# The first adaLN modulation of a hybrid trunk, summed on TensorE with the weights as the stationary operand

## The chip, the cores and the metric

The kernel runs on one core of one Trainium2 chip. The metric is the device time of one execution in microseconds, as the median of several runs. The kernel before took 2763.83 us (three runs, 2754.28 to 2770.14).

## The reference, cut to what matters

Two layers run over 256 context tokens and 512 latent tokens of width 1024. Ahead of each layer a conditioning vector, one for the latent tokens and one for the context tokens, is turned into shifts, scales and gates by one large matrix:

```python
s_lat = jax.nn.silu(c)
s_ctx = jax.nn.silu(c_ctx)
for l in range(DEPTH):
    m_lat = jnp.split((s_lat @ w_mod[l] + b_mod[l])[:, None, :], 6, axis=-1)
    m_ctx = jnp.split((s_ctx @ w_mod[l] + b_mod[l])[None, None, :], 6, axis=-1)
    h_lat = _modulate(x_lat, m_lat[0], m_lat[1])     # x * (1 + scale) + shift
    h_ctx = _modulate(x_ctx, m_ctx[0], m_ctx[1])
    ...                                              # input projection, four mixers, merge, LayerNorm, MLP
```

`w_mod[l]` is 1024 x 6144 in fp32, so this is a product of two vectors with a 25 MB matrix. Of all twelve blocks of 512 columns, layer 0 needs four (shift and scale) before its first useful product can start; the other eight, and those of layer 1, are wanted later.

## The kernel before, in words

Features lie on the 128 partitions, tokens along the free dimension. The program is written with an automatic planner: it orders each engine's instructions by priority (mostly program order), by its own idea of when operands are ready, and by free buffers; on the chip every engine and the DMA-issuing queue of SyncE (SP) then work strictly in that order. One pool tag has a fixed number of buffers, and an instruction that needs one waits until an earlier tile of the tag is released.

The vectors are made in `modulation` (L429): `ccs` holds SiLU(c) as eight columns of 128 features, two vectors side by side. One block of 512 modulation columns is summed over four quarters of 256 rows each; a quarter is 128 partitions x 2 x 512 numbers, one load. `todo` (L438) is the list of (layer, block, quarter).

Two ways of summing a block stand in the program:

- on TensorE (`first_mod`, L471 on): the load goes to tile `modw` (tag `k4`, six buffers, which the later RWKV tiles `kpad`, `ktmp`, `kr` share). The two vectors are the stationary operand (128 x 2) and the weights stream past, 512 columns at a time (L486). The sum is two rows of 512; ScalarE copies them from PSUM to `modrow` (L489), and four products with a 2 x 2 identity turn them onto the partitions (L492, tile `pq`);
- on VectorE (`mod_unit`, L447): the load goes to tile `wraw` (three buffers, shared with all weight loads of the input projection), VectorE multiplies and adds over 512 columns four times a quarter into `modacc` (L458, L460), and 16 products with a column of ones sum over the partitions (L467).

`first_mod` takes the first 16 quarters of `todo` in two parts of two blocks. In part 0 five quarters go to TensorE and three to VectorE (`fm0=5`), in part 1 six and two (`fm1=6`); a block that is split between the engines gets two additions (`add_mod`, L495). After each part `first_h` (L584) loads four input tiles `xt` (L593), scales and shifts them on VectorE (L595) and splits them into `hhi` and `hlo` (L302, L303). The first product of the input projection, r0, needs all eight; its weights are loaded after part 0 (L521). `add_mod` of part 1 is thus the last thing ahead of the second half of r0, and everything later follows from there. Later blocks of the modulation go through `mod_unit` one by one, between other work (`mod_thread`, `more_mod`).

All fp32 products of this stage (not the fp32r ones on `hhi`, `hlo`) appear in the trace as two records each. PSUM tag `fp` has two buffers.

Of the kernel before, what the change touches and what calls it, by code (L numbers as in the profile page):

```python
# [137 lines left out]
def _layout(inp):  # L138
    g = {k: np.asarray(v) for k, v in inp.items()}
    a = {}  # L140
    tok = np.concatenate([g["ctx"][0], g["x"][0]], 0)
    a["xT"] = tok.T.reshape(8, 128, T).transpose(1, 0, 2)
    i2 = np.zeros((128, 1, 2), np.float32)
    i2[0:2, 0] = np.eye(2, dtype=np.float32)
    a["cc"] = np.concatenate([np.stack([g["c"][0], g["c_ctx"]], 1).reshape(8, 128, 2).transpose(1, 0, 2), i2], 1)
    a["wmod"] = g["w_mod"].reshape(DEPTH, 4, 2, 128, 12, 512).transpose(0, 4, 1, 3, 2, 5)
    cols = _inproj_columns()
    win = np.zeros((DEPTH, NIP, 128, 8, 128), np.float32)
# [42 lines left out]
    o = SMC["w2a2"][0]  # L191
# [3 lines left out]
    o = SMC["g2"][0]  # L195
# [25 lines left out]
    i = np.arange(128)  # L221
# [14 lines left out]

PARM = (
         dict(rw0=0.3, rw1=0.1, lru=1.7, mla0=2, mla1=0.7, mlp=0.462, ml0=0.66, ml1=0.785, ga=4, sp=3, g3=10,
              g1=0.462, mod=6.6, left=219, left0=136, hr=0, hm=0, hf=0, hw=50, fm0=5, fm1=6, cs=1, dl=1, nr=1, lns=2,
              hl0=0, hl1=0, hl2=0, hres=0, hx=0, pw1=146, pw2=2, mpos=0, mstart=0),  # L240
         dict(rw0=0.099, rw1=0.3, lru=2.8, mla0=1.96, mla1=1.705, mlp=2.38, ml0=2.785, ml1=2.36, ga=2, sp=1.18,
              g3=10, g1=0.809, mod=16.8, left=146, left0=0, hr=0, hm=0, hf=0, hw=50, fm0=5, fm1=6, cs=0, dl=1, nr=0,
              lns=2, hl0=0, hl1=0, hl2=0, hres=0, hx=0, pw1=0, pw2=0, mpos=3, mstart=60),
)

# [1 line left out]
class Trunk:  # L247
# [180 lines left out]

    def modulation(self):  # L429
        nc = self.nc  # L430
        cc = self.cp.tile([128, 9, 2], F32, name="ccs")
        nc.sync.dma_start(cc, self.ins["cc"])
        ccs = cc[:, 0:8, :]
# [6 lines left out]
        self.id2 = cc[0:2, 8, :]  # L440

    def more_mod(self, n):

        for _ in range(min(n, len(self.todo))):
            self.mod_unit(*self.todo.pop(0), 0, 3)

    def mod_unit(self, l, blk, q, first, last):  # L447
# [3 lines left out]
        if q == first:  # L451
            self.acc = [self.cp.tile([128, 512], F32, tag=f"modacc{v}", name="modacc") for v in range(2)]
        for j in range(2):
            w = raw[:, 512 * j:512 * j + 512]
            for v, acc in enumerate(self.acc):
                c = self.ccs[:, 2 * q + j, v:v + 1]
                if q == first and j == 0:
# [3 lines left out]
        if q == last:  # L461
# [7 lines left out]
            self.add_mod(l, blk, pq, first > 0)  # L469

    def first_mod(self, quarters):  # L471

        nc = self.nc
        units, self.todo = self.todo[:8], self.todo[8:]
        first = quarters - 4
        ps = [self.fp("pmod") for _ in range(1 + (first > 0))]
        for q in range(4):
            for i, (l, blk, _) in enumerate((units[q], units[4 + q])):
                end = (3, first - 1)[i]
                if q > end:  # L480
                    self.mod_unit(l, blk, q, first, 3)
                    continue
                raw = self.k4("modw", (128, 2, 512))
                nc.sync.dma_start(raw, self.ins["wmod"][l, blk, q])
                for j in range(2):
                    self.mm(ps[i][0:2, :], lhsT=self.ccs[:, 2 * q + j, :], rhs=raw[:, j], start=(q + j == 0), stop=(q == end and j == 1))  # L486
                if q == end:
                    row = self.k4("modrow")[0:2, 0:512]
                    nc.scalar.activation(row, ps[i][0:2, :], AF.Copy)  # L489
                    pq = self.fp("pq")  # L490
                    for c in range(4):
                        self.mm(pq[:, 2 * c:2 * c + 2], lhsT=row[:, 128 * c:128 * c + 128], rhs=self.id2, start=True, stop=True)  # L492
                    self.add_mod(l, blk, pq, False)

    def add_mod(self, l, blk, pq, more):  # L495
        o = VEC["b_mod"][0] + 4 * blk
        m = self.mods[l][:, 4 * blk:4 * blk + 4, :]
        self.nc.vector.tensor_tensor(m, pq[:, 0:8].rearrange("p (c v) -> p c v", v=2),
                                     m if more else self.vecs[l][:, o:o + 4].unsqueeze(2).to_broadcast([128, 4, 2]), op=ALU.add)


    def layer(self, l):
        nc, tc = self.nc, self.tc
        self.l = l
        full = self.full = l < DEPTH - 1
        self.parm = PARM[0 if self.full else 1]
        with ExitStack() as ctx:
            self.phase(ctx, False)
            self.vec = self.vecs[l]
            self.mod = self.mods[l]  # L510
            if l == 0:
                nc.sync.dma_start(self.vecs[0], self.ins["vec"][0])
                for part in range(2):
                    self.first_mod(self.parm[f'fm{part}'])
                    self.first_h(part)
                    if part == 1 - self.parm['cs']:
                        nc.sync.dma_start(self.cst, self.ins["cst"])
                        for j in range(1, self.depth):
                            nc.sync.dma_start(self.vecs[j], self.ins["vec"][j])
                    if part == 0:  # L520
                        self.ahead = {IP[i]: self.load_w(self.ins["win"][0, IP[i]]) for i in ("r0",)}  # L521
            self.derived()
            self.mixers()
# [1245 lines left out]
```

## Time and profile before

| | |
|---|---|
| median of three runs | 2763.83 us |
| lowest, highest | 2754.28, 2770.14 us |
| the profiled execution | 2754.58 us, of it the profile's span 2752.8 us |
| TensorE busy | 2591.9 us (94%) |
| VectorE, ScalarE, GpSimd busy | 1538.8, 1030.2, 445.6 us |
| HBM read, written | 261.21 MB, 34.52 MB |

Read it in this way: TensorE is busy for 94% of the span, so a change pays in general only if TensorE gets its next useful product sooner. The profile's slices are 68.8 us wide, and the whole stage that the change touches lies inside the first one, so the page's strips can't resolve it; it has to be read in windows of a few microseconds and in the time-ordered list of instructions.

### The profile page before, as it was taken

To read this page: it belongs to the slowest core of one execution; us is meant where nothing else is said; L and a number is where in the kernel's file an instruction comes from. 1 tells how busy PE (TensorE), PEld (TensorE's weight loads), DVE (VectorE), ACT (ScalarE), POOL (GpSimd) and SP (SyncE) were. 2 spreads that over 40 slices of the span, in tenths; PEclk is the share of its full clock that TensorE was granted. 3 is DMA by queue.
4 is the path that set the end of the run, shared out by engine and by line. 5 is a ranking of instruction groups with operands and counts; after the bars stand their busy time and mean duration, and the time that the engine had idled before them with its cause. 6 is when DMAs were issued, how large, how long until landed. Compare 5 with 4: busy or idle time off the path is not lost. (4 is left out here: it accounts for less than half of the span.)

```text
span 2752.8 us, 53610 instructions
## 1 busy us (share of the span) xinstructions
PE 2591.9 (94%) x22980; PEld 2116.0 (77%) x22980; DVE 1538.8 (56%) x2627; ACT 1030.2 (37%) x1642; POOL 445.6 (16%) x420
## 2 busy tenths in 40 slices
PE   7999999999989999999999989889999989999997
PEld 4777776778878878888888767666777867888887
DVE  6885776643353378555552575564665346833336
ACT  3653334343222244121212466543433333623334
POOL 0111112110132131020102200121201014211111
PEclk9999999999999999999999999999998989999999
DMA  7451331132362323434332242211212455333333
GB/s 261 155 188 51 98 96 46 37 93 86 96 232 74 122 86 121 126 120 124 122 123 73 85 144 100 74 52 55 71 53 78 128 170 200 112 106 93 99 93 107
DMA packets 117294, 299.30 MB, mean 109 GB/s; under 512 B 11024, under 2 KB 38032, under 8 KB 117056
## 3 DMA queue, kind: packets, MB, share of 16 engines
q1 hardware_dynamic: 117056, 295.87, 33.7%
q8 instruction: 180, 2.95, 0.4%
q14 instruction: 58, 0.48, 0.1%
HBM read 261.21 MB, written 34.52 MB: 107 GB/s over the span
## 5 line engine op out<-in xcount | busy, mean ns | idle before, releaser
L302 ACT ACTIVATE whi<-wraw 128x1024 fp32r<-128x1024 f32 x295 | 312.2, 1058 | 954.7 <-PE m L389 758.0
L389 PE MATMUL m<-hhi,whi 128*128 128x256 f32 (+1 forms) x2000 | 600.4, 361 | 14.0 <-ACT hhi L917 3.4
L389 PE MATMUL m<-hlo,whi 128*128 128x256 f32 (+1 forms) x2000 | 591.6, 357 | 3.6 <-DVE hlo L918 2.9
L389 PE MATMUL m<-hhi,wlo 128*128 128x256 f32 (+1 forms) x2000 | 588.3, 355 | 1.4 <-issue 1.0
L303 DVE TENSOR_TENSOR wlo<-wraw,whi 128x1024 fp32r<-128x1024 f32 x291 | 364.0, 1252 | 371.0 <-ACT whi L302 359.9
L389 PEld LDWEIGHTS m<-hhi,whi 128*128 128x128 f32 x2000 | 379.2, 191 | 77.0 <-issue 8.5
L389 PEld LDWEIGHTS m<-hlo,whi 128*128 128x128 f32 x2000 | 381.2, 191 | 59.6 <-DVE hlo L918 6.2
L389 PEld LDWEIGHTS m<-hhi,wlo 128*128 128x128 f32 x2000 | 380.3, 191 | 55.5 <-issue 3.4
L460 DVE SCALAR_TENSOR_TENSOR modacc<-wraw,ccs,modacc 128x512 f32<-128x512 f32 x296 | 222.5, 800 | 34.1 <-DMA wraw<-wmod 33.8
L815 POOL TENSOR_TENSOR rl<-rl 128x512 f32<-128x512 f32 (+2 forms) x73 | 116.3, 1593 | 706.9 <-ACT rl L814 655.6
L389 PE MATMUL m<-fhi,whi 128*128 128x256 f32 (+1 forms) x608 | 176.2, 341 | 1.2 <-ACT fhi L302 1.2
L389 PE MATMUL m<-flo,whi 128*128 128x256 f32 (+1 forms) x608 | 175.6, 340 | 0.2 <-DVE flo L303 0.2
L389 PE MATMUL m<-fhi,wlo 128*128 128x256 f32 (+1 forms) x608 | 174.8, 339 | 0.0
L791 DVE SCALAR_TENSOR_TENSOR x<-m,dvec,x 128x512 f32<-128x512 f32 (+1 forms) x92 | 53.8, 606 | 130.7 <-PE m L389 130.7
L389 PEld LDWEIGHTS m<-flo,whi 128*128 128x128 f32 x608 | 114.3, 188 | 14.5 <-DVE flo L303 0.6
L389 PEld LDWEIGHTS m<-fhi,whi 128*128 128x128 f32 x608 | 114.0, 188 | 14.7 <-ACT fhi L302 1.4
L389 PEld LDWEIGHTS m<-fhi,wlo 128*128 128x128 f32 x608 | 114.2, 188 | 13.9
L716 POOL TENSOR_TENSOR gth<-gth 128x768 f32<-128x768 f32 (+1 forms) x48 | 86.7, 1827 | 228.1 <-DVE gth L712 158.4
L389 PE MATMUL m<-osp,whi 128*128 128x512 f32 (+1 forms) x384 | 102.4, 374 | 17.3 <-ACT osp L302 10.1
L303 DVE TENSOR_TENSOR flo<-rl,fhi 128x512 fp32r<-128x512 f32 (+2 forms) x73 | 54.4, 745 | 84.7 <-ACT fhi L302 84.5
L389 PEld LDWEIGHTS m<-osp,whi 128*128 128x128 f32 x384 | 68.8, 195 | 36.0 <-ACT osp L302 12.1
L302 ACT ACTIVATE fhi<-rl 128x512 fp32r<-128x512 f32 (+2 forms) x73 | 49.1, 673 | 111.7 <-POOL rl L815 111.6
(425 smaller groups left out, 4355.8 us busy)
## 6 DMA issues: line engine op xcount, KB each, us to landing
wraw<-wf SPq DMA_DIRECT2D x145, 512.0 KB, 3.5
wraw<-win SPq DMA_DIRECT2D x106, 512.0 KB, 3.7
wraw<-wmod SPq DMA_DIRECT2D x85, 512.0 KB, 3.6
wraw<-wout SPq DMA_DIRECT2D x28, 512.0 KB, 3.8
kwin<-rkv SPq DMA_DIRECT2D x20, 512.0 KB, 5.3
gd<-gth SPq DMA_DIRECT2D x22, 384.0 KB, 3.4
gth<-gd SPq DMA_DIRECT2D x22, 384.0 KB, 5.3
wraw<-wbr SPq DMA_DIRECT2D x16, 512.0 KB, 4.5
```

The lines of the kernel that those rows point to most:

```text
L302: self.nc.scalar.activation(hi, src, AF.Copy)
L303: (self.nc.gpsimd if pool else self.nc.vector).tensor_tensor(lo, src, hi.bitcast(F32), op=ALU.subtract)
L389: self.nc.tensor.matmul(out, lhsT=lhsT, rhs=rhs, start=start, stop=stop)
L460: nc.vector.scalar_tensor_tensor(acc, w, c, acc, op0=ALU.mult, op1=ALU.add)
L716: nc.gpsimd.tensor_tensor(self.z[dt][:, q0:T], self.z[dt][:, q0:T], th[:, q0:T], op=ALU.add)
L791: nc.vector.scalar_tensor_tensor(x[et][:, a:b], ps[:, a + off:b + off], gm[:, et, j:j + 1], x[et][:, a:b], op0=ALU.mult, op1=ALU.add)
L815: nc.gpsimd.tensor_tensor(rl[:, a:b], rl[:, a:b], rl[:, a:b], op=ALU.mult)
```

## The change

All 16 quarters of the first modulation go to TensorE. The weights become the stationary operand, 64 columns at a time, and the two vectors (128 x 2) stream past: per quarter 2 x 4 x 2 = 16 products of 128 x 64 with 128 x 2, which add up in PSUM directly with the features on the partitions. The copy of the rows, the turning products, the 2 x 2 identity in the input `cc`, the share of VectorE (`first`, `last`, `fm0`, `fm1`) and the second addition go. Later blocks still go through `mod_unit`, unchanged.

```diff
-    a["cc"] = np.concatenate([np.stack([g["c"][0], g["c_ctx"]], 1).reshape(8, 128, 2).transpose(1, 0, 2), i2], 1)
+    a["cc"] = np.stack([g["c"][0], g["c_ctx"]], 1).reshape(8, 128, 2).transpose(1, 0, 2)
...
-    def first_mod(self, quarters):
+    def first_mod(self):
         nc = self.nc
         units, self.todo = self.todo[:8], self.todo[8:]
-        first = quarters - 4
-        ps = [self.fp("pmod") for _ in range(1 + (first > 0))]
+        ps = [self.fp("pmod") for _ in range(2)]
         for q in range(4):
-            for i, (l, blk, _) in enumerate((units[q], units[4 + q])):
-                end = (3, first - 1)[i]
-                if q > end:
-                    self.mod_unit(l, blk, q, first, 3)
-                    continue
+            for i in range(2):
+                l, blk, _ = units[4 * i + q]
                 raw = self.k4("modw", (128, 2, 512))
                 nc.sync.dma_start(raw, self.ins["wmod"][l, blk, q])
                 for j in range(2):
-                    self.mm(ps[i][0:2, :], lhsT=self.ccs[:, 2 * q + j, :], rhs=raw[:, j], start=(q + j == 0), stop=(q == end and j == 1))
-                if q == end:
-                    row = self.k4("modrow")[0:2, 0:512]
-                    nc.scalar.activation(row, ps[i][0:2, :], AF.Copy)
-                    pq = self.fp("pq")
                     for c in range(4):
-                        self.mm(pq[:, 2 * c:2 * c + 2], lhsT=row[:, 128 * c:128 * c + 128], rhs=self.id2, start=True, stop=True)
-                    self.add_mod(l, blk, pq, False)
+                        for e in range(2):
+                            o = 128 * c + 64 * e
+                            self.mm(ps[i][64 * e:64 * e + 64, 2 * c:2 * c + 2], lhsT=raw[:, j, o:o + 64], rhs=self.ccs[:, 2 * q + j, :],
+                                    start=(q + j + c == 0), stop=(q == 3 and j == 1 and c == 3))
+                if q == 3:
+                    self.add_mod(l, blk, ps[i])
...
-                    self.first_mod(self.parm[f'fm{part}'])
+                    self.first_mod()
```

## Rows read from the trace of the kernel before

**Rows 1.** The page, its first part: busy time of the engines over the span.

```profile
PE 2591.9 (94%) x22980; PEld 2116.0 (77%) x22980; DVE 1538.8 (56%) x2627; ACT 1030.2 (37%) x1642; POOL 445.6 (16%) x420
```

**Rows 2.** Long windows: stretch and its length, then busy us (and count) of PE, PEld, DVE, ACT, POOL, then PEclk, DMA share, GB/s.

```profile
0.00:48.65 48.65, 34.87 (x164) 13.52 (x164) 26.66 (x90) 13.74 (x20) 0.78 (x15) 0.92 0.83 318
48.65:54.00 5.35, 4.92 (x14) 3.93 (x15) 5.35 (x10) 3.30 (x4) 0.00 (x0) 0.50 0.00 0
...
60.00:80.00 20.00, 19.66 (x130) 15.96 (x129) 19.33 (x30) 9.67 (x12) 1.55 (x4) 1.00 0.58 188
```

**Rows 3.** Windows of 2 us in the first 50 us, columns as in group 2.

```profile
2.00:4.00 2.00, 0.00 (x0) 0.00 (x0) 0.00 (x0) 0.23 (x2) 0.00 (x0) 1.00 0.63 135
4.00:6.00 2.00, 0.17 (x1) 0.12 (x2) 1.15 (x13) 0.97 (x2) 0.00 (x0) 1.00 1.02 397
...
22.00:24.00 2.00, 0.11 (x4) 0.02 (x2) 1.84 (x10) 0.51 (x1) 0.00 (x0) 0.83 1.03 412
...
26.00:28.00 2.00, 2.00 (x3) 0.25 (x2) 2.00 (x3) 0.01 (x1) 0.00 (x0) 0.50 1.03 410
...
38.00:40.00 2.00, 2.00 (x13) 1.57 (x11) 1.72 (x3) 0.00 (x0) 0.00 (x0) 1.00 0.75 302
...
46.00:48.00 2.00, 0.40 (x14) 0.31 (x12) 1.52 (x6) 0.24 (x1) 0.00 (x0) 0.80 0.00 0
```

**Rows 4.** Timeline, first 50 us: start us, us, engine, line, operation, count, idle before and releaser.

```profile
5.83 5.48 PE L389 MATMUL pmod<-modw,ccs 128*2 128x512 f32 x8 [5.83 <-DMA modw<-wmod]
...
14.04 5.31 PE L389 MATMUL pmod<-modw,ccs 128*2 128x512 f32 x12 [1.00 <-DMA modw<-wmod]
...
21.01 1.10 PE L389 MATMUL pq<-one,modacc 128*64 128x1 f32 x32
...
25.84 9.15 PE L389 MATMUL pmod<-modw,ccs 128*2 128x512 f32 x16
...
36.98 2.74 DVE L460 SCALAR_TENSOR_TENSOR modacc<-wraw,ccs,modacc 128x512 f32<-128x512 f32 x4
...
40.05 3.59 PE L389 MATMUL pmod<-modw,ccs 128*2 128x512 f32 x8
...
43.68 0.59 ACT L489 ACTIVATE modrow<-pmod 2x512 f32<-2x512 f32 x1 [8.06 <-DMA lruw<-lruw]
...
44.32 1.05 PE L389 MATMUL pq<-ccs,modrow 2*128 2x2 f32 x8
...
45.30 1.10 PE L389 MATMUL pq<-one,modacc 128*64 128x1 f32 x32
...
46.45 0.17 DVE L498 TENSOR_TENSOR mod<-pq,mod 128x8 f32<-128x8 f32 x1 [0.87 <-PE pq L389]
...
48.65 1.01 PE L389 MATMUL m<-hhi,whi 128*128 128x256 f32 x2 [2.25 <-ACT hhi L302]
```

**Rows 5.** Timeline of the SP queue: start of issue, time in issue, line, tile, count.

```profile
22.20 7.58 SPq L484 DMA_DIRECT2D modw<-wmod  x2
...
33.21 2.64 SPq L450 DMA_DIRECT2D wraw<-wmod  x2
...
40.13 0.42 SPq L954 DMA_DIRECT2D lruw<-lruw  x1
55.88 0.33 SPq L450 DMA_DIRECT2D wraw<-wmod  x1
```

**Rows 6.** Loads of the first 70 us: line, size of one, median time to landing.

```profile
modw<-wmod SPq DMA_DIRECT2D x11, 512.0 KB, 11.1
...
xt<-xT SPq DMA_DIRECT2D x8, 384.0 KB, 8.0
...
cst<-cst SPq DMA_DIRECT2D x1, 865.0 KB
```

**Rows 7.** PE by shape at 2106 us, and the window with its granted clock, columns as in group 2.

```profile
L389 PE MATMUL kpx<-kS,kKR 64*64 64x64 f32 x16 | 1.1, 318 | 0.0
...
2106.00:2108.00 2.00, 2.00 (x26) 1.82 (x26) 0.74 (x3) 0.54 (x2) 0.00 (x0) 0.50 0.00 0
```

More of the change, by code (lines that the diff above doesn't have):

```diff
@@ L142, in _layout @@
     a["xT"] = tok.T.reshape(8, 128, T).transpose(1, 0, 2)
-    i2 = np.zeros((128, 1, 2), np.float32)
-    i2[0:2, 0] = np.eye(2, dtype=np.float32)
-    a["cc"] = np.concatenate([np.stack([g["c"][0], g["c_ctx"]], 1).reshape(8, 128, 2).transpose(1, 0, 2), i2], 1)
+    a["cc"] = np.stack([g["c"][0], g["c_ctx"]], 1).reshape(8, 128, 2).transpose(1, 0, 2)
     a["wmod"] = g["w_mod"].reshape(DEPTH, 4, 2, 128, 12, 512).transpose(0, 4, 1, 3, 2, 5)
@@ L238 @@
          dict(rw0=0.3, rw1=0.1, lru=1.7, mla0=2, mla1=0.7, mlp=0.462, ml0=0.66, ml1=0.785, ga=4, sp=3, g3=10,
-              g1=0.462, mod=6.6, left=219, left0=136, hr=0, hm=0, hf=0, hw=50, fm0=5, fm1=6, cs=1, dl=1, nr=1, lns=2,
+              g1=0.462, mod=6.6, left=219, left0=136, hr=0, hm=0, hf=0, hw=50, cs=1, dl=1, nr=1, lns=2,
               hl0=0, hl1=0, hl2=0, hres=0, hx=0, pw1=146, pw2=2, mpos=0, mstart=0),
          dict(rw0=0.099, rw1=0.3, lru=2.8, mla0=1.96, mla1=1.705, mlp=2.38, ml0=2.785, ml1=2.36, ga=2, sp=1.18,
-              g3=10, g1=0.809, mod=16.8, left=146, left0=0, hr=0, hm=0, hf=0, hw=50, fm0=5, fm1=6, cs=0, dl=1, nr=0,
+              g3=10, g1=0.809, mod=16.8, left=146, left0=0, hr=0, hm=0, hf=0, hw=50, cs=0, dl=1, nr=0,
               lns=2, hl0=0, hl1=0, hl2=0, hres=0, hx=0, pw1=0, pw2=0, mpos=3, mstart=60),
@@ L430, in modulation @@
         nc = self.nc
-        cc = self.cp.tile([128, 9, 2], F32, name="ccs")
-        nc.sync.dma_start(cc, self.ins["cc"])
-        ccs = cc[:, 0:8, :]
+        ccs = self.cp.tile([128, 8, 2], F32, name="ccs")
+        nc.sync.dma_start(ccs, self.ins["cc"])
         th = self.cp.tile([128, 8, 2], F32, name="ccth")
@@ L439, in modulation, with mod_unit @@
         self.ccs = ccs
-        self.id2 = cc[0:2, 8, :]
     def more_mod(self, n):
         for _ in range(min(n, len(self.todo))):
-            self.mod_unit(*self.todo.pop(0), 0, 3)
-    def mod_unit(self, l, blk, q, first, last):
+            self.mod_unit(*self.todo.pop(0))
+    def mod_unit(self, l, blk, q):
         nc = self.nc
@@ L450, in mod_unit @@
         nc.sync.dma_start(raw, self.ins["wmod"][l, blk, q])
-        if q == first:
+        if q == 0:
             self.acc = [self.cp.tile([128, 512], F32, tag=f"modacc{v}", name="modacc") for v in range(2)]
@@ L456, in mod_unit @@
                 c = self.ccs[:, 2 * q + j, v:v + 1]
-                if q == first and j == 0:
+                if q + j == 0:
                     nc.vector.tensor_scalar(acc, w, c, 0.0, op0=ALU.mult, op1=ALU.add)
@@ L460, in mod_unit @@
                     nc.vector.scalar_tensor_tensor(acc, w, c, acc, op0=ALU.mult, op1=ALU.add)
-        if q == last:
+        if q == 3:
             pq = self.fp("pq")
@@ L468, in mod_unit @@
                                 lhsT=acc[:, 128 * c + 64 * e:128 * c + 64 * e + 64], rhs=self.one, start=True, stop=True)
-            self.add_mod(l, blk, pq, first > 0)
-    def first_mod(self, quarters):
+            self.add_mod(l, blk, pq)
+    def first_mod(self):
         nc = self.nc
         units, self.todo = self.todo[:8], self.todo[8:]
-        first = quarters - 4
-        ps = [self.fp("pmod") for _ in range(1 + (first > 0))]
+        ps = [self.fp("pmod") for _ in range(2)]
         for q in range(4):
-            for i, (l, blk, _) in enumerate((units[q], units[4 + q])):
-                end = (3, first - 1)[i]
-                if q > end:
-                    self.mod_unit(l, blk, q, first, 3)
-                    continue
+            for i in range(2):
+                l, blk, _ = units[4 * i + q]
                 raw = self.k4("modw", (128, 2, 512))
@@ L485, in first_mod, with add_mod @@
                 for j in range(2):
-                    self.mm(ps[i][0:2, :], lhsT=self.ccs[:, 2 * q + j, :], rhs=raw[:, j], start=(q + j == 0), stop=(q == end and j == 1))
-                if q == end:
-                    row = self.k4("modrow")[0:2, 0:512]
-                    nc.scalar.activation(row, ps[i][0:2, :], AF.Copy)
-                    pq = self.fp("pq")
-                    for c in range(4):
-                        self.mm(pq[:, 2 * c:2 * c + 2], lhsT=row[:, 128 * c:128 * c + 128], rhs=self.id2, start=True, stop=True)
-                    self.add_mod(l, blk, pq, False)
-    def add_mod(self, l, blk, pq, more):
+                    for c in range(4):
+                        for e in range(2):
+                            o = 128 * c + 64 * e
+                            self.mm(ps[i][64 * e:64 * e + 64, 2 * c:2 * c + 2], lhsT=raw[:, j, o:o + 64], rhs=self.ccs[:, 2 * q + j, :],
+                                    start=(q + j + c == 0), stop=(q == 3 and j == 1 and c == 3))
+                if q == 3:
+                    self.add_mod(l, blk, ps[i])
+    def add_mod(self, l, blk, pq):
         o = VEC["b_mod"][0] + 4 * blk
@@ L498, in add_mod @@
         self.nc.vector.tensor_tensor(m, pq[:, 0:8].rearrange("p (c v) -> p c v", v=2),
-                                     m if more else self.vecs[l][:, o:o + 4].unsqueeze(2).to_broadcast([128, 4, 2]), op=ALU.add)
+                                     self.vecs[l][:, o:o + 4].unsqueeze(2).to_broadcast([128, 4, 2]), op=ALU.add)
     def layer(self, l):
```

## The prediction, made before the change was run

> **What bounds the kernel now.** I read the page's busy times first: TensorE is busy 2591.9 of 2752.8 us [rows 1], so a change elsewhere helps only where TensorE waits or does needless work. The chain of waits reaches back no further than the second layer, so for the start I took windows. Up to 48.65 us TensorE counts 34.87 us as busy; from 60 to 80 us it is busy for 19.66 of 20 us and VectorE for 19.33 of 20 [rows 2]. So the kernel is throughput bound from the moment the second half of r0 starts, at 48.65 us, and the question is what sets that moment.
>
> The time-ordered list answers it [rows 4]. Most of TensorE's "busy" time in the start is the first modulation with two stationary columns: 5.48 + 5.31 + 9.15 + 3.59 = 23.5 us. The chain that ends last is all in series: the last two quarters 40.05 to 43.64, the row copy on ScalarE to 44.27, the turning products from 44.32, the products with ones to 46.40, the addition to 46.62, then 2.03 us of VectorE and ScalarE until the first wide product on the new half of `h` at 48.65. VectorE's own quarters (the last sums end at 39.72) are earlier, so its sums are not what is late.
>
> The second thing to see is the memory. From 4 us on the loads run at about 410 GB/s, DMA share 1.02 or more, and they fall off only in 38 to 40 us [rows 3]. A quarter is 512 KB, an `xt` 384 KB, `cst` 865 KB [rows 6]: 1.28, 0.96 and 2.16 us at that rate. The 135 and 397 GB/s of the windows up to 6 us are 1.07 MB, so full rate began in effect at 3.4 us. Sixteen quarters, eight `xt`, `cst`, the vectors, r0's weights and the loads that came with them (`mml`, `smr`, two later quarters) are 14.6 MB, and 3.4 + 14.6 / 0.41 = 39 us: the window where the rate fell. This check lets me use bytes as a clock for landings.
>
> **The change, part by part.** *The products.* A quarter becomes 16 products, 32 records, each with a fresh 128 x 64 load and two columns streamed. The nearest row is the sum over `modacc`: same 128 x 64 stationary, one column, 32 records in 1.10 us [rows 4]. So 1.10 us a quarter at full clock, against 3.59 / 2 = 1.80 us now at full clock and 9.15 / 4 = 2.29 where half of the stretch had the clock at 0.50 [rows 3, 4].
>
> *The clock.* It fell in 22 to 24 and in 46 to 48 us, means 0.83 and 0.80 [rows 3]; both times the last thing TensorE had done were the small `pq` products [rows 4]. The new stage consists of such products, so I expect 0.50 (1.2 GHz) for most of it. No row shows a product with one or two columns at that level. The nearest is `kpx`, 16 records with 64 stationary and 64 streamed columns, 1.1 us at 0.50 [rows 7]: 69 ns a record, 2.2 us a quarter. Bounds 1.10 and 2.2; I take 1.3, near the lower, since `modacc` has the same stationary and nearly the same streamed width, while half of `kpx`'s columns are streamed ones that the new product hasn't. The Trainium skill (TensorE: Matmul & The Clock Gate, section LDWEIGHTS) gives the load as its columns divided by 1.2 GHz, an estimate of 53 ns for 64 columns and 1.71 us a quarter; it speaks against reloading for every two columns. The trace's 32 loads with their products in 1.10 us are quicker than that, at full clock; at the half clock nothing here shows it. By that page the sum below would come out as in the third rival, at a smaller price.
>
> *Removed from the chain's end.* Row copy 0.59, turning 1.05, products with ones 1.10, with the small steps 46.40 - 43.64 = 2.76 us; the second addition too. VectorE's sums, `id2` and the smaller `cc` I cost at nothing: they lie beside TensorE's work now.
>
> *Moved: the loads.* All 16 quarters now need the six `k4` buffers, so from the seventh on a load waits in SP until TensorE has consumed an earlier quarter, and `xt`, r0's weights, `cst` and the next `wraw` loads are queued behind. Such waits exist already: SP spent 7.58 us on two `modw` issues [rows 5]. They cost nothing while the loads in flight cover them: a `modw` lands 11.1 us after issue [rows 6], six buffers are 7.7 us of transfer, and TensorE at 1.3 us a quarter gives them back as fast as they arrive. If that cover is gone (2.2 us a quarter) the loads run at TensorE's pace, the third rival. Against this, loads that don't need `k4` may slip ahead of the last quarters and push them back.
>
> *When the last quarter lands.* By bytes: only the quarters, `cc` and the first vectors (8.47 MB) give 24.1 us; with four `xt`, `cst`, the second vectors and r0's weights (11.5 MB) 31.5; with all eight `xt` (13.1 MB) 35.3; with everything 39. I take the second and half of the later `xt`, 12.3 MB: 33.4 us.
>
> *TensorE's lag.* Between part 0 and the end of part 1 TensorE must also do the first half of r0: 24 wide records, 5 to 8 us by the clock (in the trace before they filled most of 36.8 to 40.0). With eight quarters at 1.3 us that is 15 to 18 us, in the some 17 us that the loads leave, so I add 1 us. Part 1 ends at 33.4 + 1.3 + 1 = 35.7, the addition at 35.9, and with the same 2.03 us the second half of r0 starts at 38.0 instead of 48.65 us.
>
> **The sum.** 48.65 - 38.0 = 10.6 us. After that point the same work follows in the same program order, at a mean DMA load far under the rate of the start, so I carry the gain on in full. The profiled execution took 2754.58 us and becomes 2744.0. It was almost the lowest of the runs shown; their median is 9.25 us higher, and on that scale, which I forecast, it is 2763.8 - 10.6 = 2753.2 us. Half a per cent, about what a measurement of this kernel can tell from no change, is 13.8 us: the forecast counts as "within".
>
> **The rivals.** *First, more than that.* If the planner places the quarters ahead of `cst` and of the later `xt` (landing 24 to 31 us) and the lag vanishes, r0 goes on at 28 to 35 us, a gain of 14 to 21. For it: VectorE, which is full from 48.65 us on (5.35 of 5.35, then 19.33 of 20) [rows 2], is freed of five quarters' sums, 2.74 us each [rows 4], in the start, and could there do later quarters that now crowd the stretch behind; a load of `wraw` was issued only at 55.88 us, 15 us after the load before it [rows 5]. Against: six buffers can't hold sixteen quarters, so something must slip between. Mid price 17 us, 2746.8 us.
>
> *Second, the forecast itself is sensitive to order:* landing between 31.5 and 39 us and a lag of 0 to 3 us give gains of 3 to 13.8, 2750 to 2761 us.
>
> *Third, TensorE paced by half-clock reloads.* At `kpx`'s 2.2 us a quarter, 16 x 2.2 = 35.8 us from 5.83 on, with r0's first half (6.5 us) in between: 48.1, addition and 2.03 us make 50.4, 1.7 us later than now: 2765.5 us. For it: the clock falls behind small products [rows 3]. Against: TensorE's wide products in between would lift it, and `modacc` has the nearer shape. With the skill's figure in place of that row it would be 16 x 1.71 + 5.83 + 6.5 = 39.7, r0 at 41.9 us, 2757 us.
>
> *Fourth, slower.* The planner orders everything behind from its own clock, and the start that it sees changes. TensorE's idle time is 160.9 us, 13.8 of it before 48.65 [rows 1, 2], so 147 us lie in the mixers and the second half, where the order of later modulation quarters and weight loads on SP decides. From the point where this idle time grows by 10.6 the gain is gone; from 24.4 us, a sixth, it is slower by over 0.5%, 2778 us. Nothing in the program order behind the stage changes, which speaks against so much.
>
> That the change doesn't do what it says would show as `modrow` or `modacc` in the first 40 us; the diff leaves no way for it.
>
> **How the numbers follow.** Forecast with its order band 0.53, first rival 0.27, third 0.12, fourth 0.08. Faster by over 0.5%: the first rival and a little of the band's upper edge, 0.30; slower 0.07, as the fourth may stop short of the bound; within 0.63. Eight in ten: from a gain of 21 with some 5 us of the runs' own spread below, 2738 us, to the third rival with a little of the fourth, 2768 us.
>
> **What would show it.** Right: `pmod` in records of 128 x 64 with 128 x 2, no `modrow`, 512 of them and under 25 us in sum; the granted clock at 0.50 over most of the first 30 us; DMA at about 410 GB/s until 35 us or more; the last of the four additions near 36 and the first wide product on the second half of `h` near 38 us; beyond that the same stretches, about 10 us earlier. Wrong in price if 32 records take 2 us; wrong in the load order if the DMA windows show gaps while SP waits on `pmod`; wrong in the carry if r0 comes 10 us sooner and the end doesn't.

## The result and the profile after

| | before | after |
|---|---|---|
| median of 20 runs each, side by side | 2765.67 us | 2784.22 us |
| lowest, highest | 2753.82, 2782.23 | 2765.39, 2788.63 |
| ratio after / before, 95% interval | | 1.0056 (1.004 to 1.0073) |
| profiled execution, its span | 2754.58, 2752.8 | 2782.65, 2780.9 |

The change makes the kernel slower by 0.56%, some 15.5 us (11 to 20) by the ratio; the medians lie 18.6 us apart. I had forecast 10.6 us faster.

The window table of the changed kernel, columns as in [rows 2] and [rows 3]:

```profile
0.00:54.50 54.50, 37.22 (x536) 34.17 (x536) 12.42 (x58) 10.68 (x14) 0.77 (x15) 1.00 0.76 285
...
30.00:32.00 2.00, 0.93 (x2) 0.50 (x2) 1.35 (x4) 1.02 (x2) 0.00 (x0) 1.00 0.05 20
32.00:34.00 2.00, 2.00 (x34) 1.98 (x34) 0.28 (x1) 0.00 (x0) 0.00 (x0) 1.00 0.00 0
36.00:38.00 2.00, 2.00 (x26) 1.90 (x27) 0.00 (x0) 0.00 (x0) 0.00 (x0) 1.00 0.44 174
46.00:48.00 2.00, 2.00 (x15) 1.40 (x15) 0.00 (x0) 0.00 (x0) 0.00 (x0) 1.00 1.03 422
```

From 30 to 34 us memory all but stands still, with half of the modulation's products still to come; in the kernel before it ran at 393 and 377 GB/s there. The time-ordered list says why (start us, us, engine, line, operation, count, idle before and releaser; `mm` is now L387, the split L300):

```profile
6.00 13.82 PE L387 MATMUL pmod<-ccs,modw 128*64 128x2 f32 x256 [6.00 <-DMA modw<-wmod]
...
16.05 21.59 SPq L476 DMA_DIRECT2D modw<-wmod  x8
...
24.69 1.82 ACT L300 ACTIVATE hhi<-xt 128x768 fp32r<-128x768 f32 x2 [1.70 <-DVE xt L587]
...
26.54 1.28 ACT L549 ACT_TABLE_LOAD   x1
...
28.48 1.28 ACT L550 ACT_TABLE_LOAD   x1
...
29.98 1.04 ACT L300 ACTIVATE whi<-wraw 128x1024 fp32r<-128x1024 f32 x1
...
31.07 1.01 PE L387 MATMUL m<-hhi,whi 128*128 128x256 f32 x2 [11.24 <-ACT whi L300]
...
32.01 1.88 PE L387 MATMUL pmod<-ccs,modw 128*64 128x2 f32 x32
...
33.82 1.01 PE L387 MATMUL m<-hlo,whi 128*128 128x256 f32 x2
...
35.40 1.88 PE L387 MATMUL pmod<-ccs,modw 128*64 128x2 f32 x32
...
47.48 7.00 PE L387 MATMUL pmod<-ccs,modw 128*64 128x2 f32 x128
...
54.52 0.17 DVE L490 TENSOR_TENSOR mod<-pmod,vec 128x8 f32<-128x8 f32 x1 [1.54 <-PE pmod L387]
...
56.73 1.01 PE L387 MATMUL m<-hhi,whi 128*128 128x256 f32 x2 [2.25 <-ACT hhi L300]
...
63.88 0.48 ACT L1380 ACTIVATE kpad<-m,dvec 128x256 f32<-128x256 f32 x1 [2.71 <-PE m L387]
...
65.61 1.06 ACT L300 ACTIVATE whi<-wraw 128x1024 fp32r<-128x1024 f32 x1
...
66.72 0.61 PE L387 MATMUL m<-hhi,whi 128*128 128x256 f32 x2 [2.88 <-ACT whi L300]
```

Read it in four steps. Part 0 ends at 19.82 us. TensorE then stands for 11.24 us in front of r0's first wide product, which the planner queued ahead of part 1; part 1's weights are in their buffers behind it. That product waits for r0's split, which stands on ScalarE behind the splits of `h`, two table loads and derived vectors. SP can't issue part 1's other quarters while the buffers are held: 21.59 us in issue. And all that follows, 24 wide records and eight quarters, runs in series at half clock (0.84 us a pair of wide records, where 0.51 is the pair at full clock; why the clock column still reads 1.00 is told with the wide products below): 54.50 - 31.07 = 23.4 us. The second half of r0 starts at 56.73 us, 8.1 later than in [rows 4]. Later the second product waits 2.88 us for its weights' split, which stands behind r0's elementwise work (65.61 us); in the kernel before that split came ahead of it (52.79 us).

As a mark further on I use the start of the tenth product of `h` with a block of projection weights, the same product in all kernels. TensorE's timeline of the changed kernel:

```profile
157.86 0.91 PE L387 MATMUL m<-hhi,whi 128*128 128x256 f32 x2
```

and of the kernel before:

```profile
143.88 0.92 PE L389 MATMUL m<-hhi,whi 128*128 128x256 f32 x2
```

In a second profile of each (below) the mark stands at 157.80 and at 148.75 us. At the second half of r0 the two pairs of profiles are 8.1 and 5.6 us apart, at the mark 14.0 and 9.0. So the first 160 us hold a loss of 9.0 to 14.0 us, more than half of the 15.5. What is lost behind the mark isn't a new order: from 150 us on the load queue, ScalarE and VectorE of the first two profiles go through the same tiles in the same order. (The expectations below take the 10th split of weights on ScalarE, counted from 0, as their mark; it stood at 147.18 and 132.03 us in these two profiles, at 146.99 and 137.17 in the second ones.)

### The profile page after: what moved, and what is told of

Read it like the earlier page. It is cut to its first block, busy times and chain, and to the rows that moved or that the text cites. A ratio compares the mean times of both kernels' runs of the same rounds, so it can differ in the third digit from the quotient of the medians.

```text
span 2780.9 us, 54328 instructions
## 1 busy us (share of the span) xinstructions
PE 2612.6 (94%) x23352; PEld 2149.5 (77%) x23352; DVE 1531.0 (55%) x2605; ACT 1028.1 (37%) x1638; POOL 443.7 (16%) x420
## 5 line engine op out<-in xcount | busy, mean ns | idle before, releaser
L300 ACT ACTIVATE whi<-wraw 128x1024 fp32r<-128x1024 f32 x295 | 312.2, 1058 | 955.8 <-PE m L387 762.4
L387 PE MATMUL m<-hhi,whi 128*128 128x256 f32 (+1 forms) x2000 | 604.2, 363 | 24.0 <-ACT whi L300 14.1
L387 PE MATMUL m<-hlo,whi 128*128 128x256 f32 (+1 forms) x2000 | 594.6, 358 | 2.0 <-DVE hlo L910 1.9
L387 PE MATMUL m<-hhi,wlo 128*128 128x256 f32 (+1 forms) x2000 | 592.4, 357 | 1.3 <-DVE wlo L301 1.3
L387 PEld LDWEIGHTS m<-hhi,whi 128*128 128x128 f32 x2000 | 381.2, 193 | 86.9 <-ACT whi L300 14.5
L387 PEld LDWEIGHTS m<-hlo,whi 128*128 128x128 f32 x2000 | 383.4, 192 | 58.6 <-DVE hlo L910 4.9
L387 PEld LDWEIGHTS m<-hhi,wlo 128*128 128x128 f32 x2000 | 382.7, 192 | 55.8 <-issue 2.6
L456 DVE SCALAR_TENSOR_TENSOR modacc<-wraw,ccs,modacc 128x512 f32<-128x512 f32 x280 | 213.5, 811 | 42.8 <-DMA wraw<-wmod 42.8
L387 PE MATMUL m<-fhi,whi 128*128 128x256 f32 (+1 forms) x608 | 176.2, 341 | 1.2 <-ACT fhi L300 1.2
L387 PE MATMUL m<-flo,whi 128*128 128x256 f32 (+1 forms) x608 | 175.7, 340 | 0.2 <-DVE flo L301 0.2
L387 PE MATMUL m<-fhi,wlo 128*128 128x256 f32 (+1 forms) x608 | 174.9, 339 | 0.0
L387 PEld LDWEIGHTS m<-flo,whi 128*128 128x128 f32 x608 | 114.3, 188 | 14.7 <-DVE flo L301 0.8
L387 PEld LDWEIGHTS m<-fhi,whi 128*128 128x128 f32 x608 | 114.0, 188 | 14.7 <-ACT fhi L300 1.4
L387 PEld LDWEIGHTS m<-fhi,wlo 128*128 128x128 f32 x608 | 114.2, 188 | 13.9
L387 PE MATMUL m<-osp,whi 128*128 128x512 f32 (+1 forms) x384 | 101.4, 371 | 17.6 <-ACT osp L300 10.4
L387 PEld LDWEIGHTS m<-osp,whi 128*128 128x128 f32 x384 | 68.3, 194 | 36.3 <-ACT osp L300 12.3
L300 ACT ACTIVATE fhi<-rl 128x512 fp32r<-128x512 f32 (+2 forms) x73 | 49.1, 673 | 111.5 <-POOL rl L807 111.5
```

The costliest lines, as they stand in the source:

```text
L300: self.nc.scalar.activation(hi, src, AF.Copy)
L387: self.nc.tensor.matmul(out, lhsT=lhsT, rhs=rhs, start=start, stop=stop)
```

## The experiments

Of the experiments' runs beside the kernel before, the ratio is given with its 95% interval.

**r0's weights first.** The load of r0's weights goes ahead of both parts.

```diff
+                self.ahead = {IP[i]: self.load_w(self.ins["win"][0, IP[i]]) for i in ("r0",)}
                 for part in range(2):
                     self.first_mod()
...
-                    if part == 0:
-                        self.ahead = {IP[i]: self.load_w(self.ins["win"][0, IP[i]]) for i in ("r0",)}
```

> r0's weights are loaded before the first quarter, so their split no longer stands on ScalarE behind the derived vectors. In the changed kernel TensorE idled 11.2 us (19.8 to 31.1) until that split. Theory 1, the loss in the start is this wait on the path: the wait shrinks to some 3 us (the split of the first halves of h), and the second half of r0 starts at 46 to 49 us instead of 56.7; the whole run about 8 us below the changed kernel's 2784, near 2775. Theory 2, part 1 is held by the loads (six buffers) or by the price of the narrow products alone, and the wait only fills time that would be lost anyway: the second half of r0 stays at 55 to 57 us and the time at 2784.

Measured: ratio 1.003 (1.0005 to 1.0056), median 2773.13 us. TensorE's timeline:

```profile
7.47 13.82 PE L387 MATMUL pmod<-ccs,modw 128*64 128x2 f32 x256 [7.47 <-DMA modw<-wmod]
23.54 1.01 PE L387 MATMUL m<-hhi,whi 128*128 128x256 f32 x2 [2.24 <-ACT hhi L300]
...
30.09 10.02 PE L387 MATMUL pmod<-ccs,modw 128*64 128x2 f32 x256
...
42.35 1.01 PE L387 MATMUL m<-hhi,whi 128*128 128x256 f32 x2 [2.24 <-ACT hhi L300]
...
52.62 1.01 PE L387 MATMUL m<-hhi,whi 128*128 128x256 f32 x2 [2.88 <-ACT whi L300]
```

Two windows of part 1, columns as in [rows 2]:

```profile
32.00:34.00 2.00, 2.00 (x75) 2.00 (x74) 0.01 (x1) 0.00 (x0) 0.27 (x6) 1.00 0.88 219
36.00:38.00 2.00, 2.00 (x42) 2.00 (x42) 0.00 (x0) 0.00 (x0) 0.16 (x3) 0.50 0.94 247
```

The 11 us wait is gone, so its cause was the place of r0's split. The second half of r0 comes at 42.35 us, earlier than the 46 to 49 expected and 6.3 earlier than before. The price of a record goes with the granted clock. The windows also count records that only reach into them, so 2 us / 75 and 2 us / 42 come out too low; from start to start the trace has 29 ns at 1.00 (30.2 to 34.6 us), 53 ns at 0.50 (35.0 to 39.9 us), and 53 ns in part 0 (13.82 us / 256 is 54, with the last record's own time in it). The expectation for 128 columns below still goes by 27 ns. But the 6.3 us don't last: the second product starts at 52.62 us, against about 55.8 in the kernel before, waits again for a split, and ends at 64.6 against 65.1.

**r0's weights last.** The same load goes behind part 1 (`if part == 1`), so that r0 isn't in part 1's way.

> r0's weights are loaded after part 1, so TensorE does all 256 narrow products of both parts in a row and all of r0 behind them. Theory 1 (wait for r0's split on the path, narrow products at 54 ns a record as in the changed kernel): 16 quarters at 1.73 us from 6 us on end at 34 to 36 us, the second half of h can be used from 37 to 39 us; r0, wholly at half clock (48 wide records, 16.8 us), ends near 52 to 54 us, against 63.8 in the changed kernel and 56.0 in the kernel before; time near 2772. Theory 2 (the loads hold part 1 because only six buffers are there): gaps of TensorE between quarters and SP waiting on narrow products; part 1 ends after 42 us and r0 after 58, time near 2780.

Measured: ratio 1.0019 (0.9999 to 1.0038), median 2767.01 us. TensorE's timeline:

```profile
24.18 13.82 PE L387 MATMUL pmod<-ccs,modw 128*64 128x2 f32 x256 [3.93 <-DMA modw<-wmod]
44.71 1.01 PE L387 MATMUL m<-hhi,whi 128*128 128x256 f32 x2 [6.70 <-ACT whi L300]
```

Part 1 ends at 38.0 instead of the 34 to 36 us expected: there was a wait for a load, and the products took 13.82 us again. r0 starts with all of `h` at 44.71 and ends at 55.5 us (52 to 54 expected), where the kernel before ended at 56.0. Ahead of it TensorE waited 6.70 us for the split of its weights, which now came last.

**More buffers too.** As the last, with the second block's quarters in the ring of the projection weights, so that nine buffers serve.

```diff
-                raw = self.k4("modw", (128, 2, 512))
+                if i:
+                    raw = self.wp.tile([128, 2, 512], F32, tag="wraw", bufs=NW[0], name="modx")
+                else:
+                    raw = self.k4("modw", (128, 2, 512))
```

> As with r0 loaded late, but the second block's quarters go to the three weight buffers instead of the six shared ones, so nine loads can be under way. If the loads hold part 1: it ends at least 2 us earlier than with r0 late alone, and SP's waits on narrow products shrink. If TensorE's pace holds it (1.73 us a quarter, the loads need 1.28): the same within 1 us, and the time the same within the runs' spread.

Measured: ratio 1.0011 (0.999 to 1.0032), median 2765.27 us. Part 1 ends 0.9 us earlier (37.1), and r0 starts at 43.77; the first product of part 0 was 0.9 us earlier already (5.52 against 6.43 us). The six buffers were not what cost: part 1 is paced by TensorE's 1.73 us a quarter.

**A wide product among the narrow ones.** Per half quarter one more product, two stationary columns and 512 streamed ones, whose sum nobody reads.

```diff
                 for j in range(2):
+                    self.mm(self.wps[0:2, :], lhsT=self.ccs[:, 2 * q + j, :], rhs=raw[:, j], start=True, stop=True)
                     for c in range(4):
```

> The changed kernel with one extra product of 512 streamed columns (fp32, two records) for each half quarter, whose result is not used: it measures what the narrow records cost at the higher clock. If the price of the narrow products depends on the granted clock: behind the point where wide records drop from 0.43 us to 0.22 us, 32 narrow records take 0.9 to 1.1 us instead of 1.75. If it doesn't: 1.75 us at either level. Part 0 ends later than 19.8 us in either case (at 22 to 30 us), as 32 wide records are added to it.

One execution, 2829.4 us. It doesn't answer its question, since the clock didn't rise. TensorE's timeline of one half quarter:

```profile
7.88 1.02 PE L387 MATMUL pmod<-ccs,modw 128*64 128x2 f32 x16
8.83 1.86 PE L387 MATMUL warm<-modw,ccs 128*2 128x512 f32 x2
```

and a long window, columns as in [rows 2]:

```profile
8.00:60.00 52.00, 48.79 (x326) 18.95 (x327) 9.33 (x30) 6.20 (x8) 0.00 (x0) 1.00 0.48 165
```

0.93 us for a record of 512 columns is twice the 3.59 / 8 = 0.45 of [rows 4], and it stays so for 52 us in which TensorE is busy for 48.79. The granted clock's first entry comes only at 102.75 us; before it the column reads 1.00, whatever the products took. At that entry the wide records of r0 do fall from 0.84 to 0.52 us a pair, so the entry is right and only the time ahead of it isn't. The Trainium skill (TensorE: Matmul & The Clock Gate, section Seeing it yourself) warns that records of the clock have been unreliable; here it is the stretch before the first record that misleads. The column says nothing about the first 62 us of the changed kernel either (its first entry stands at 62.19 us), and I go there by durations.

**Both kernels again.** Nothing is edited; one more profile of each.

> The kernel before, profiled a second time. The changed kernels gained or lost their time in the first 150 us, but then all five of them were 9 to 12 us longer than the profile of before between the 20th and the 25th split of input weights (before 145.5 us with 6 us at the half level of the clock, the others 154.5 to 157.6 us with 25 to 33 us). Theory A: the profile of before (2754.58 us, against a median of 2765.67) happened to miss half-clock stretches that every version has there; then this second profile shows 20 to 33 us at 0.50 in that stage, the stage takes 152 to 158 us, and the execution takes 2760 to 2770. Rival B: the changed start brings those stretches on, by what it leaves behind for the clock; then this profile again has under 10 us at 0.50 there and the stage takes 145 to 148 us.

> The changed kernel, profiled a second time. The loss at the start is the order of TensorE's queue and of ScalarE's, which is written into the program: both theories expect the wait for r0's first weights (11.2 us) again within 0.5 us, part 1's last product at 54 to 55 and r0's end at 63 to 65. Theory A (half-clock stretches later on come and go from execution to execution) expects the stage between the 20th and 25th split of input weights to differ from its 154.5 us by 3 us or more in one of the two new profiles; rival B (the start decides them) expects 153 to 156 again.

2772.04 and 2783.55 us. The changed kernel's start repeats: the wait, and the mark at 157.80. The stage from the 20th to the 25th split took 151.4 us with 24 us at half clock in the second profile of before, 145.5 with 6 in the first, and 155.1 in the second of the changed kernel. Theory A's figures for the kernel before were missed by a little (152 us and 2760 to 2770 us expected), and the changed kernel's stage repeated, as the rival had it. So 5.9 of the 9.0 us between the first profiles were those of one execution, and 3.7 us stay. The window over that stage in the first profile of before, columns as in [rows 2]:

```profile
363.00:515.00 152.00, 141.59 (x2879) 107.94 (x2878) 92.53 (x233) 61.62 (x153) 27.11 (x34) 0.98 0.17 53
```

and in the second, with the granted clock at 0.93 instead of 0.98:

```profile
363.00:515.00 152.00, 141.18 (x2787) 108.04 (x2788) 89.87 (x218) 56.95 (x140) 27.87 (x34) 0.93 0.18 57
```

Over all executions the mean granted clock was 0.970 for the changed kernel (21) and 0.970 for the one before (81), at mean spans of 2780.0 and 2761.9 us: some 168 and 167 us at half clock by the column. But the column counts nothing ahead of its first entry, which the changed kernel has at 62 us and the one before at 8 to 10 us; up to 65 us it counts none in the former and 13.7 and 17.1 us in the two profiles of the latter. If the other executions' starts are like these, equal means leave the changed kernel some 15 us more at half clock behind its start, and its two profiles show more there: 177.8 and 172.4 us behind 65 us, against 127.1 and 156.0. Over the 81 executions of the kernel before the span grows by 0.40 us for each us at half clock, so I estimate some 6 us of the loss from it. What brings this time on, no run shows.

**Both first weights early.** r0's and `lru0`'s weights are loaded between part 0's quarters and its `xt`.

```diff
                     self.first_mod()
+                    if part == 0:
+                        self.ahead = {IP[i]: self.load_w(self.ins["win"][0, IP[i]]) for i in ("r0", "lru0")}
                     self.first_h(part)
...
-                    if part == 0:
-                        self.ahead = {IP[i]: self.load_w(self.ins["win"][0, IP[i]]) for i in ("r0",)}
```

> The changed kernel with the weights of the first two wide products (r0 and lru0) loaded between part 0's quarters and its inputs, ahead of the inputs instead of behind, so that both are split before the inputs are and TensorE has two products' first halves to work on while part 1's quarters arrive. Theory (the loss is the wait for two weight splits that stand behind other work on ScalarE): no wait over 3 us ahead of r0's first wide product, which starts at 23 to 25; the clock rises at 27 to 29 and then stays up longer, so that part 1's products cost 0.9 us a quarter where they run at full clock; second product's end at 52 to 57 against 65.1 before, and a start 7 to 12 us shorter than before, so 2754 to 2764 by the median if nothing after it changes, ratio 0.995 to 0.998. Rival (what the start leaves behind costs half-clock time later): start as said, but ratio 0.999 to 1.003. Rival (narrow products among wide ones keep the clock low): clock falls again before 40 us and part 1 costs 1.7 us a quarter, second product's end at 60 to 65, ratio about 1.000.

Measured: ratio 1.0029 (1.0004 to 1.0054), median 2772.89 us. The start is about as the theory says up to the second product, whose end is 57.3 us against 65.1. Then, in the timeline of SP, TensorE and VectorE:

```profile
54.67 0.33 SPq L341 DMA_DIRECT2D wraw<-win  x1
...
59.40 0.62 PE L387 MATMUL m<-hhi,whi 128*128 128x256 f32 x2 [2.09 <-ACT whi L300]
...
61.35 1.22 DVE L301 TENSOR_TENSOR wlo<-wraw,whi 128x1024 fp32r<-128x1024 f32 x1
...
62.62 1.01 PE L387 MATMUL m<-hhi,wlo 128*128 128x256 f32 x2 [2.25 <-DVE wlo L301]
```

The third product's weights were issued at 54.67 us, behind three quarters of the later modulation that had taken the ring's buffers, and their low part stands on VectorE behind that modulation's sums. TensorE waits twice, falls to half clock (0.84 us a pair of records instead of 0.51), and the third product ends at 72.8, against 73.6 before. A gain of 7.8 us is gone within one product.

**128 columns a load.** As the last, with one product of 128 stationary columns in place of two of 64.

```diff
-                        for e in range(2):
-                            o = 128 * c + 64 * e
-                            self.mm(ps[i][64 * e:64 * e + 64, 2 * c:2 * c + 2], lhsT=raw[:, j, o:o + 64], ...)
+                        o = 128 * c
+                        self.mm(ps[i][:, 2 * c:2 * c + 2], lhsT=raw[:, j, o:o + 128], ...)
```

> As both_weights_early, with each stationary operand 128 columns wide instead of 64: half as many products and reloads for the same weights (128 in all for a part, 8 for a quarter). At the half level of the clock a 64-column record took 54 ns in part 0, at the full level 27 ns. Theory (price by columns: one column per cycle of the granted clock): 107 ns a record at half clock, 54 at full, a quarter again 1.73 us, part 0 again 13.8 us, and the whole within 2 us of both_weights_early. Rival (price per instruction): 54 ns a record, a quarter 0.87 us, part 0 then paced by its loads (last quarter landing about 18 us, end at 18 to 19 instead of 21), and 1 to 4 us faster than both_weights_early.

Measured: ratio 1.0114 (1.0078 to 1.0149), median 2794.58 us. TensorE's timeline of part 0, which took 13.82 us with 64 columns (the profile is that of the longest execution, 2818.41 us):

```profile
5.94 27.44 PE L387 MATMUL pmod<-ccs,modw 128*128 128x2 f32 x128 [5.94 <-DMA modw<-wmod]
```

27.44 us / 128 = 214 ns a record: neither 107 (by columns) nor 54 (by instruction), but four times the price for twice the columns. Both expectations fell. Later in the trace such records start every 213 ns where the clock is 0.50 (57 to 69 us) and every 112 ns where it is 1.00 (44 to 50 us), again four times the 29 ns of 64 columns; those start in pairs there, 6 to 7 ns apart and 58 ns from pair to pair, while the 128-column ones start one by one. Why stays open: that consecutive products of 64 columns write to different halves of the output partitions is a candidate, which was not tested.

**The later modulation held back.** In the planner's parameters of layer 0 the later modulation's thread starts 20 us later. Done with both weights early, with the kernel before, with the changed kernel, and with r0 late and more buffers.

```diff
-              hl0=0, hl1=0, hl2=0, hres=0, hx=0, pw1=146, pw2=2, mpos=0, mstart=0),
+              hl0=0, hl1=0, hl2=0, hres=0, hx=0, pw1=146, pw2=2, mpos=0, mstart=20),
```

> As both_weights_early, with the later modulation's first quarter held back in the planner by 20 us (its thread's start 0 -> 20), so that the third product's weights stand in the load queue ahead of two quarters of that modulation instead of behind them. In both_weights_early the second wide product ended at 57.3 us, 7.8 us earlier than in the profile of before, and nothing of that was left at the third one's end (72.8 against 73.6): its weights were issued at 54.67 and their low part was split at 61.35, behind the later modulation's sums on VectorE, and TensorE waited 2.09 and 2.25 us and fell to half clock. Theory (the start's gain is lost in that queue): third product starts within 1 us of the second one's end and ends at 65 to 67; the 10th split of weights comes at 124 to 130 us (132.0 and 137.2 in the two profiles of before, 136.3 in both_weights_early) and the ratio to before is 0.995 to 0.999. Rival (the elementwise chain of the first recurrent unit, lru, holds the next products wherever the third one stands): third product as said, but 10th split at 131 to 137 and ratio 0.999 to 1.003.

> The kernel before with the same held-back modulation thread (0 -> 20) and nothing else, so that what both_early_mods_later gains can be put down to the early weights or to the planner's new order. If the gain is the early weights': this one is within 0.15% of before (ratio 0.9985 to 1.0015), 10th split at 130 to 137. If it is the planner's order: as fast as both_early_mods_later. If holding the modulation back costs something later: ratio over 1.002.

> The changed kernel with the later modulation's thread held back (0 -> 20) as in before_mods_later, and nothing else: the fourth corner of a square of before/after and 0/20. Theory (the change's loss is TensorE's wait for r0's weights in the first 64 us, and the planner's order later on is a separate matter): the wait of 11 us ahead of r0's first wide product is there again, r0 ends at 63 to 65, the 10th split of weights comes at 137 to 143 us (126.6 in before_mods_later), and the ratio to before is 1.001 to 1.004, that is 13 to 20 us over before_mods_later. Rival (the change loses by the order that the planner draws up behind it): the ratio comes to within 0.1% of before_mods_later's 0.9968.

> late_more_buffers (r0's weights behind part 1, half of the quarters in a second ring of buffers) with the modulation's thread held back (0 -> 20). Theory: part 1 ends at 37 and r0 starts at 43 to 44 as before; the second weights are now split ahead of r0's elementwise work, so the second product follows the first at 53 to 55 and ends at 62 to 64 (65.1 in the profile of before, 58.0 in both_early_mods_later); the 10th split at 122 to 126 us, ratio 0.994 to 0.997. Rival (a start that leaves TensorE idle for 7 us ahead of r0 keeps the clock low longer and eats the gain): second product's end at 65 to 67, 10th split at 127 to 130, ratio 0.997 to 0.999.

| kernel | modulation from 0: ratio | mark | from 20 us: ratio | mark |
|---|---|---|---|---|
| before | 1 | 143.88, 148.75 | 0.9968 (0.9945 to 0.9991) | 140.09 |
| after | 1.0056 (1.004 to 1.0073) | 157.86, 157.80 | 1.0012 (0.999 to 1.0034) | 146.50 |
| both weights early | 1.0029 (1.0004 to 1.0054) | 147.20 | 0.9961 (0.9934 to 0.9989) | 133.86 |
| r0 late, more buffers | 1.0011 (0.999 to 1.0032) | 140.49 | 0.9965 (0.9942 to 0.9988) | 138.92 |

The medians of the right half are 2753.89, 2764.52, 2754.32 and 2750.44 us. TensorE's timeline of the changed kernel with the modulation held back:

```profile
31.37 1.01 PE L387 MATMUL m<-hhi,whi 128*128 128x256 f32 x2 [11.24 <-ACT whi L300]
...
54.32 1.01 PE L387 MATMUL m<-hhi,whi 128*128 128x256 f32 x2 [2.25 <-ACT hhi L300]
```

Three things follow. The changed kernel keeps its wait of 11.24 us and stays slower than the one before under the new order too, by 0.0044 of the time, 12 us; the wait is the change's own. r0 ends at 60.9 us (63 to 65 expected) and the 10th split came at 133.05 us (137 to 143 expected); the second product no longer waits behind r0. Second, the gain of 0.3 to 0.4% belongs to the order that the planner draws up with the thread held back, since the kernel before gets it with one number. That number moves far more than the first loads: the kernel before's load queue changes in 33 places and ScalarE's order in 61, as far as 913 us. With r0 late the second product ended at 63.1 us without it and at 64.0 with it, and the mark moved by 1.6 us only while the time moved by some 13 (to about 9), so most of that gain seems to lie behind the mark; which of the changed places it comes from is not shown. With both weights early the start is 13.3 us shorter for it (147.20 to 133.86), and the third product follows the second at 57.8 us and ends at 66.5; with r0 late the second product ends at 64.0 us, both as expected (the first one's 10th split, at 120.41, comes even earlier than the 124 to 130 us expected, the second one's, at 125.47, as expected). Third, three kernels now beat the original by a little, and the narrow products in the best order are not measurably faster than the old ones in the same order: 0.9961 and 0.9965 against 0.9968, each to about 0.0025. With both weights early the mark came 6.2 us sooner, in single profiles, than in the kernel before under the same order (133.86 against 140.09), and yet the medians are 2754.32 and 2753.89 us.

## Why the prediction was wrong

**What bounds the kernel.** That the start ends when part 1's sum does, and that the second half of r0 is the moment to watch, holds. "Throughput bound from 48.65 us on" doesn't: the full windows of [rows 2] hid that the next products wait for splits and loads in a fixed order. With both weights early TensorE came 7.8 us sooner to that point, and waited.

**The price of a quarter.** I took 1.3 us between 1.10 and 2.2. Part 0 measured 13.82 / 8 = 1.73 us. I had leaned on the nearest shape, `modacc` in [rows 4], and gave too little weight to its clock, which was the full one. At full clock the new records cost the same as those of `modacc`, one every 29 ns in both traces: 0.93 us a quarter in a row, under my lower bound, as the 1.10 us of `modacc` are 31 steps of 29 ns and 0.20 us for the last record. The Trainium skill (TensorE: Matmul & The Clock Gate, section LDWEIGHTS) gave an estimate of 53 ns for 64 columns; part 0's 53 ns agrees, the 29 ns at the 2.4 GHz level with r0's weights first don't, and 128 columns at 214 ns are twice the 107 that it gives as an estimate. This term was worth 16 x 0.43 = 6.9 us in the time to the last product.

**The clock.** Right, by the products' durations, that it would be 0.50 over the start (the column, which I had named as the sign, reads 1.00 there); wrong that TensorE's wide products would lift it. In the changed kernel the 24 wide records between narrow ones took 0.84 us a pair, half clock, to the end.

**The removed chain.** Right: no row copy, turning or second addition, no sums on VectorE. The addition is followed by the same 2.2 us until the wide product (54.52 to 56.73).

**The loads and TensorE's lag.** This step failed most. I added 1 us of lag, after counting TensorE's work and not its queue. The kernel before has the same wait, only shorter; its timeline of ScalarE and TensorE:

```profile
24.24 1.04 ACT L302 ACTIVATE whi<-wraw 128x1024 fp32r<-128x1024 f32 x1
25.33 0.58 PE L389 MATMUL m<-hhi,whi 128*128 128x256 f32 x1 [3.22 <-ACT whi L302]
```

I passed over these 3.22 us, and never asked where ScalarE would put that split when the work around it moved. It came at 29.98 and cost 11.24 us; the loads, which were my clock for landings, then stopped for TensorE, as the prediction's own test said they would show: no traffic while SP waits for `pmod`. The third rival, TensorE paced by reloads, was the nearest one. (Its sum as I wrote it is off: 16 x 2.2 is 35.2, not 35.8, so r0 at 49.8, 1.1 us later than before.) With 1.73 us a quarter it gives 6.0 + 16 x 1.73 + r0's first half, which took 23.4 - 13.8 = 9.6 us at half clock, = 43.3; the wait of 11.24 makes 54.5, which is what was measured.

**The carry.** I carried 10.6 us on in full. The loss at r0, 8.1 and 5.6 us in the two pairs of profiles, didn't go on unchanged but grew to 14.0 and 9.0 at the mark, and gains of 6.3 and 7.8 us in two experiments vanished in the next product or the one after. Even where the second and third weights stood well in the queues, 6.2 us at the mark didn't show in the median.

**The rivals.** The fourth had the right cause, order from the planner, at the wrong place: it looked behind the start, where the order stayed as it was; what was lost there goes by my estimate with half-clock time. None of the four put a wait in TensorE's own queue. "Slower by over 0.5%" had a chance of 0.07.

Not settled: after and before under the new order differ by 12 us (to about 9) in the ratios, by 6.4 in the marks. The kernels with r0 early ended at or near the start of before and were 0.3% slower. For r0's weights first the executions on record bear on it: their mean granted clock is 0.967 (12) against 0.970 in the kernel before beside them (29), some 19 us more at half clock, which at 0.40 us each is an estimate of 7.6 us for the 7.9 between the mean spans. For both weights early the means are 0.968 and 0.969, and most of its loss stays open. Whether the start brings the half-clock time on was not tested.

## What to carry to other kernels

Follow every operation that is made cheaper or moved through each in-order queue: what stands ahead of each operand of TensorE's next instruction, on ScalarE and in the load queue too, counts for more than how much work there is; here one number that redraws the planner's order was worth 0.3%, and the rewritten sum nothing measurable in the same order. When operands are swapped so that few columns stream, price the stationary loads from a row at the clock level that the new stage will have. And before a gain at a stage's end is carried on, look whether the weights of the next two or three products are loaded and split by then, and count the half-clock time behind it over all executions, not in one profile.

## What the runs showed of the hardware

- Products with a fresh fp32 stationary load and two streamed columns, from start to start: 53 ns for 64 columns at 1.2 GHz and 29 ns at 2.4 GHz, but 213 and 112 ns for 128 columns.
- A stream of such products, even with wide ones of two stationary columns in between that keep TensorE busy for 48.79 of 52 us, didn't bring the higher clock level. By themselves the same wide products were what TensorE did before the level rose at 9.7 us in the kernel before; with r0's weights first the level rose at 27.9 us, in the sixth pair of products with 128 stationary columns after part 0.
- The column of the granted clock reads 1.00 until its first entry (62 us in the changed kernel, 102.75 with the wide products), while the products run at half speed.
- Over 81 executions of the kernel before, the span grew by 0.40 us for each us at half clock (twice the clock's missing share of the span).
